# Odd attention: the low keys of each map in a tile of 128 rows, half of them zero

## The chip, the cores and the metric

The kernel runs on one core of a Trainium2 chip. The metric is device time of one execution in microseconds (us). A core has TensorE (PE; its weight loads are shown as PEld), VectorE (DVE), ScalarE (ACT), GpSimd (POOL) and SyncE (SP), which here only issues transfers. Each engine takes its instructions in program order; they wait for each other by semaphores.

## The reference

A float32 model of three layers for 512 tokens of 1024 features. The first layer mixes with two softmax attentions and the second with differential attention (the odd mixer); each is followed by a gated feed-forward network with a convolution. The third has a gated delta rule and a squared-relu network. The change touches the differential attention alone. It has 8 heads; each has two maps of queries and keys of 64 features and one set of values of 128:

```python
l1 = jnp.einsum('bqhd,bkhd->bhqk', q1b, k1).astype(jnp.float32) * scale + alibi
l2 = jnp.einsum('bqhd,bkhd->bhqk', q2b, k2).astype(jnp.float32) * scale + alibi
p = (jax.nn.softmax(jnp.where(mask, l1, NEG_INF), axis=-1)
     - lam * jax.nn.softmax(jnp.where(mask, l2, NEG_INF), axis=-1)).astype(v.dtype)
return jnp.einsum('bhqk,bkhd->bqhd', p, v)
```

The output of each head goes through an RMS norm, and all heads through one projection of 1024 x 1024.

## The kernel before, in words

Every large product works on float32r, a form of float32 that holds fewer bits. An operand is split exactly into a high part (a copy, by ScalarE) and a low part (the difference, by VectorE or at some places GpSimd), and a product is the sum of three: high x high, high x low, low x high (`mm3`, L171 to L175). Weights come by DMA of 512 KB into one of two raw tiles and are split into one of four pairs `whi`, `wlo`.

The stage of the odd attention works head by head. For each head `project` (L921) makes keys and queries of both maps, features on the 128 partitions: map 0 in rows 0 to 63 and map 1 in rows 64 to 127. There are 16 steps of three products (the tile `kq`), and they are not done at once but serve as filling: `fill(n)` puts a few of them between the steps of the head before, whose chain of softmax work they cover.

A score is the sum of the same three parts, but with 64 features two of them fit into one product. For map m the tile `qs[:, m]` holds the queries' high part in m's own 64 rows (`r`) and their low part in the other 64 (`ro`); `ks[:, m]` holds the keys' high part in both halves. One product over all 128 rows (L966, the high product) gives high x high + low x high. The third part, the queries' high part by the keys' low part, is a second product (L967, the low product) that adds into the same bank. Before the change it takes the 64 rows `r` alone, of `qs` and of a tile `kl` in which both maps' low keys lie one above the other; `kl` has two buffers, used by the heads in turn.

`scores(qb)` (L959) does this for one block of 128 queries, for map 0 and then map 1, with 256, 256, 384 and 512 columns of keys for the blocks 0 to 3. Each score then goes through one operation on VectorE (L970: the position's bias and the row's minimum), an exponential on ScalarE (L971), the combination of both maps on VectorE (`combine`, L980 to L983), transposes on TensorE (`turn_P`, L392), a copy on ScalarE, and the product with the values (`pv`, L992). The head's output is normed (GpSimd, L1005 to L1008), scaled (`o`, L1014), transposed (`ot`, L1019) and split in the course of the next head.

The order of all this on TensorE, ScalarE and VectorE is written out by hand (L1040 to L1115, `manual_schedule`). The keys' low parts of the next head are written by `k_lo` (L938), directly after `scores(3)`. In the last head there are no next keys, and products of the output's projection (`o`) serve as filling. GpSimd splits one weight tile a head, copies the keys' high part to the other half (L936) and makes the bias (L953).

Of the kernel before, what the change touches and what calls it, by code (L numbers as in the profile page):

```python
# [19 lines left out]
S = 512  # L20
D = 1024
P = 128
# [15 lines left out]
class Out:  # L38
    """tokens @ W for 1024 output columns, each block's halves in two of the eight banks, chunk by chunk"""
# [25 lines left out]
def parts(hi, lo):  # L65
    """chunk k of a feature-major pair, for the tokens of block t"""
    return lambda k, t: (hi[:, k, t * P:(t + 1) * P], lo[:, k, t * P:(t + 1) * P])


class Kern:  # L70
# [22 lines left out]
    def open_x(self):  # L93
        """the residual stream and the scratch beside it, at the far end of SBUF"""
        self.xp = self.tc.alloc_tile_pool(name="xp", bufs=1, side="right", reuse_waits="tile")
        self.sp = self.xp
        self.x = self.xp.tile([P, NT, D], F32, name="x")
# [18 lines left out]
    def ps(self, tag, name="ps"):  # L116
        """one PSUM bank; each of the four tags rotates over two"""
        return self.psum.tile([P, 512], F32, tag=tag, name=name, bufs=2)
# [8 lines left out]
    def junk(self):  # L127
        """where squares go that only their sums are wanted of"""
        return self.sp.tile([P, D], BF16, tag="junk", name="junk")

    @contextmanager
    def smalls(self, pool):
        """small tiles come from this phase's pool meanwhile"""
        kept, self.small = self.small, pool
        yield pool
        self.small = kept
# [9 lines left out]
    def split(self, hi, lo, src, eng=None):  # L146
        """src = hi + lo exactly; hi and lo are float32r."""
        i = self.nc.scalar.copy(hi, src)
        return i.ins, (eng or self.nc.vector).tensor_tensor(lo, src, hi.bitcast(F32), ALU.subtract).ins
# [14 lines left out]
    def wsteps(self, raw, n=1024, eng=None):  # L164
        """a weight tile's high part, and the step that makes its low part"""
# [11 lines left out]
    def lnexp(self):  # L177
        """from here on the scalar engine's Exp and Ln come from one table set"""
        self.tc.keep_in_program_order(self.nc.scalar.preload_act_table_set("natural_log_exp_and_others"))

    def rstd(self, ss, n, name="rstd"):
        """1 / sqrt(ss / n + eps) for a small tile of sums of squares."""
# [14 lines left out]
    def scale(self, t):  # L197
        """1 / rms of block t of x"""
# [4 lines left out]
    def prenorm(self, i):  # L203
        """rms_norm of x with gain i, into feature-major parts in hT, in steps for block t"""
# [29 lines left out]
    def postnorm_add(self, gain_row):  # L234
        """x[t] += rms_norm(ps) * gain, ps: two banks of 512 columns; in steps for proj_out"""
# [37 lines left out]
    def proj_A(self, ps, w, M, nk, rhs, cols=slice(0, S), woff=0):  # L273
        """ps[:M, cols] = W_tile^T @ rhs; W tile is [P, nk, M], features land on partitions"""
# [8 lines left out]
    def proj_B(self, ps, t, ws, kper, N, lhs, ks=None, nk=KC):  # L283
        """ps[:, :N] = tokens of block t @ W; W tiles are [P, kper, N]"""
# [7 lines left out]
    def proj_out(self, out, finish, nxt=None, tail=4):  # L292
        """tokens @ W for 1024 output columns; the last `tail` chunks go block by block.
        finish: steps that take a block's sums; nxt: what follows, (i, head): the norm before it, and the
        weights (source, columns) and the products of what goes ahead with two blocks. Or a function of t"""
# [90 lines left out]
    def transpose_P(self, PT, Pt, qb, name, copy=None):  # L386
        """PT[:, kb, qb block] = Pt[:, kb block]^T for kb <= qb"""
# [10 lines left out]
    def head_pair(self, pp, score, v, vcol):  # L398
        """softmax(causal(scores)) v of two heads in stages, by query block and head; score(ps, qb, j, n): the products"""
# [31 lines left out]
        def pv():  # L431
            """(P v)^T, one head in each half of the array's columns"""
# [9 lines left out]
    def even_mixer(self, gain_post, nxt):  # L442
        nc, a = self.nc, self.a
        with self.pool("ev_o") as op_:
            # outputs: fox heads as parts, MLA heads for now as they are
# [13 lines left out]
    def _even_attention(self, pp, fox, oT, out):  # L459
# [7 lines left out]
        # running sums of the forget gates: parts, and those of their negatives  # L467
# [5 lines left out]
        # fox values, token-major  # L473
# [11 lines left out]
        # fox heads' parts, two heads at a time: high and low above one another; high parts of the keys twice;  # L485
        # high parts of the queries and low parts of the keys, under them the gates' sums' parts against ones
# [13 lines left out]
        # shared rotary keys and forget gates  # L500
# [72 lines left out]
        # compressed queries and keys, normed token-major, then feature-major  # L573
# [38 lines left out]
        def flat(blocks, late=None):  # L612
            """the blocks' products and sums of squares; what follows apart or, with some that are late, behind six
            products of the next block"""
# [15 lines left out]
        # (the rotations' tables carry the scale)  # L630
# [9 lines left out]
        class Head2:  # L640
            """the queries and keys of two MLA heads"""
# [46 lines left out]
        with self.tc.manual_schedule(engines={E.PE, E.Activation, E.DVE}):  # L688
            # fox heads
# [106 lines left out]
        # MLA heads; a pair's last transposes and its products with the values are in the next one  # L796
# [82 lines left out]
    def _odd_attention(self, pp, ohi, olo, out):  # L879
# [32 lines left out]

        ws, w_lo = {}, [nothing] * 20
# [7 lines left out]
        def project(h):  # L921
            """steps to the parts of both maps' keys and queries: keys' high parts twice, queries' parts one
            above the other"""
            qs = pp.tile([P, 2, S], F32R, tag="qs", name="qs", bufs=2)
            ks = pp.tile([P, 2, S], F32R, tag="ks", name="ks", bufs=2)
            kl = pp.tile([P, S], F32R, tag="kl", name="kl", bufs=2)
            heads[h] = qs, ks, kl
# [10 lines left out]
            def k_lo():  # L938
                for m, (r, ro) in enumerate(rows):
                    nc.vector.tensor_tensor(kl[r], pk[r], ks.bitcast(F32)[r, m, :], ALU.subtract)  # L940
# [8 lines left out]
        def attend(h):  # L949
            """scores (negative) and probabilities, in stages: scores by block, transposes by block, products by block"""  # L950
            qs, ks, kl = heads[h]
# [7 lines left out]
            def scores(qb, between=nothing):  # L959
# [4 lines left out]
                for m in range(2):  # L964
                    ps = self.ps("a", "sc")
                    mm(ps[:, :w], qs[:, m, qb * P:(qb + 1) * P], ks[:, m, :w], start=True, stop=False)  # L966
                    mm(ps[:, :w], qs[rows[m][0], m, qb * P:(qb + 1) * P], kl[rows[m][0], :w], start=False, stop=True)  # L967
# [30 lines left out]
            def norm():  # L998
                # rms_norm of po / den
# [118 lines left out]
    def head_A(self, srcs):  # L1118
        """the first half of the tokens for the first four tiles of features"""
# [12 lines left out]
    def head_B(self, srcs):  # L1132
        """the first two blocks of a token-major product"""
# [6 lines left out]
    def head_block(self, t, ws=None):  # L1140
        """block t of a token-major product, from the head if it is there"""
# [6 lines left out]
    def dn_head(self):  # L1148
        """halves of the gates' tile and of the first keys and queries"""
# [49 lines left out]
    def deltanet(self, nxt):  # L1199
        nc, a = self.nc, self.a  # L1200
        self.spill_x()
        with self.pool("dn_o") as op_:
            # w and the decayed q of each block; then, in their place, the parts of its gated outputs
# [4 lines left out]
            with self.pool("dn") as pp, self.smalls(pp):  # L1208
                hd = [dict(h=h, wq=[w[:, h] for w in wq]) for h in range(8)]
                with self.pool("dn_t") as tp:  # L1210
# [5 lines left out]
                    # v, then u, then the outputs  # L1216
# [24 lines left out]
    def _dn_tail(self, sp, pp, st, hd, new_parts, nw):  # L1241
        """u and w, the scan over the chunks, gates, and the outputs' parts"""
# [7 lines left out]
        # q's scale 1 / sqrt((|q|^2 + eps) dk) goes to the outputs  # L1250
# [13 lines left out]
        # what the scan's waits are filled with, and the number of blocks it needs the parts of  # L1264
# [47 lines left out]
    def _dn_gates(self, tp, pp, st):  # L1312
        """per-token decay and step sizes of all heads, token-major [P, block, head]"""
# [50 lines left out]
        def soft(y, sign, out):  # L1364
            """out = max(sign*y, 0) + ln(1 + exp(-|y|))"""
# [31 lines left out]
        # rows of gc, as exact bfloat16 parts, for broadcasting over partitions  # L1397
# [12 lines left out]
        # and of its exponential  # L1410
# [8 lines left out]
    def _dn_conv(self, st, h, i, c):  # L1419
        """projection and causal convolution of one head's q, k or v, feature-major"""  # L1420
# [16 lines left out]
    def _dn_qk(self, tp, pp, st, d):  # L1437
# [11 lines left out]
        # products of keys with keys and queries, and of queries, within the chunks  # L1449
# [10 lines left out]
        # sums of squares per token lie on the diagonals  # L1460
# [6 lines left out]
        # rho = beta / (|k|^2 + eps), in logarithms  # L1467
# [6 lines left out]
        # decays within the chunks, masked: [key, block, query in its chunk]  # L1474
# [8 lines left out]
        # decayed queries  # L1483
# [23 lines left out]
    def _dn_solve(self, tp, st):  # L1507
        """inverses of the 32-wide unit triangles on the diagonals, one per partition"""
# [14 lines left out]
        # columns of the inverse are independent: two engines take some each  # L1523
# [14 lines left out]
    def _dn_post(self, tp, pp, st, d):  # L1538
        """inverses of the 64-wide triangles from those of their halves, then u and w"""
# [78 lines left out]
    def _dn_z(self, sp, t, ws):  # L1618
        """silu of the gates' projection for four heads of a block"""
# [18 lines left out]
    def _dn_norm(self, sp, st, t, half):  # L1638
        """scales of four heads' outputs in a block: the norm's joined with q's"""
# [13 lines left out]
    def _dn_parts(self, st, t, half, z, r, gp, nw):  # L1653
        """the parts of rms_norm(o) * silu(z) for four heads of a block, feature-major"""
# [39 lines left out]
def build(nc, tc, a):  # L1694
    with ExitStack() as ctx:
# [40 lines left out]
        def final(t, ps):  # L1736
            """out = rms_norm(x + ps), by halves"""
# [19 lines left out]
def pack_A(w, cols):  # L1757
    """[K, N] -> tile [128, K/128 * len(cols)]: W[k*128+p, cols[c]] at [p, k, c]"""
# [5 lines left out]
def pack_B(w, kper):  # L1764
    """[K, N] -> tiles [K/(128 kper), 128, kper*N]"""
# [46 lines left out]
def pack(inp):  # L1812
# [6 lines left out]
    # layer 0  # L1819
# [20 lines left out]
    # layer 1  # L1840
# [6 lines left out]
    # FFN  # L1847
# [6 lines left out]
    # gated deltanet and MLP  # L1854
# [28 lines left out]
```

## Time and profile before

| what | value |
|---|---|
| timed runs | 1982.19 us median of 3 (1981.41 to 1982.5) |
| profiled execution | span 1982.6 us; the record has no time beside the span |
| TensorE busy | 1951.9 us, 98% |
| weight loads busy | 1587.0 us, 80% |
| VectorE, ScalarE, GpSimd busy | 1011.6, 823.1, 253.0 us |
| chain that ended last | 84% TensorE |
| stage of the odd attention | 705.7 to 866.1 us |

The busy time of TensorE counts matmuls whose ends are modelled, and a matmul's end overlaps the start of the next. How long one holds the engine is therefore read from its start to the start of the next. The notation 64*128 64x256 in a row means 64 rows by 128 columns of the array, and a moving operand of 64 x 256.

### The profile page before, as it was taken

To read this page: it belongs to the slowest core of one execution; us is meant where nothing else is said; L and a number is where in the kernel's file an instruction comes from. 1 tells how busy PE (TensorE), PEld (TensorE's weight loads), DVE (VectorE), ACT (ScalarE), POOL (GpSimd) and SP (SyncE) were. 2 spreads that over 40 slices of the span, in tenths; PEclk is the share of its full clock that TensorE was granted. 3 is DMA by queue.
4 is the path that set the end of the run, shared out by engine and by line. 5 is a ranking of instruction groups with operands and counts; after the bars stand their busy time and mean duration, and the time that the engine had idled before them with its cause. 6 is when DMAs were issued, how large, how long until landed. Compare 5 with 4: busy or idle time off the path is not lost.

```text
span 1982.6 us, 25298 instructions
## 1 busy us (share of the span) xinstructions
PE 1951.9 (98%) x9960; PEld 1587.0 (80%) x9960; DVE 1011.6 (51%) x1663; ACT 823.1 (42%) x1411; POOL 253.0 (13%) x336
## 2 busy tenths in 40 slices
PE   8999999999999999999999999999999999999998
PEld 6787688888888777778888888888778888888886
DVE  5666665444323546747444432577764645324423
ACT  4656544333313455645333321476532334313322
POOL 0213210000000233311000000100353310000000
PEclk9999999999999999999999999999999999999999
DMA  5111133322221411123323322323330143322322
GB/s 172 58 65 64 43 108 109 103 97 96 96 96 64 136 54 48 60 75 108 98 97 102 96 96 88 113 98 103 93 96 1 51 141 107 96 96 96 96 96 75
DMA packets 51643, 177.76 MB, mean 90 GB/s; under 512 B 7188, under 2 KB 8084, under 8 KB 51396
## 3 DMA queue, kind: packets, MB, share of 16 engines
q1 hardware_dynamic: 50068, 173.38, 26.7%
q0 software_dynamic: 1456, 2.76, 0.5%
q8 instruction: 79, 1.29, 0.3%
q14 instruction: 40, 0.33, 0.0%
HBM read 170.28 MB, written 5.77 MB: 89 GB/s over the span
## 4 chain that ended last, share of the span: by engine, by line
PE 84%; DVE 4%; ACT 2%; issue 1%; DMA 1%; POOL 0%; POOLq 0%; ACTq 0%; DVEq 0%
PE o L173 9%; PE o L174 9%; PE o L175 9%; PE gate L173 4%; PE val L175 4%; PE val L173 4%; PE gate L175 4%; PE gate L174 4%; PE val L174 4%; PE up L175 3%; PE up L174 3%; PE up L173 3%; PE kq L173 2%; PE dproj L173 2%; PE dproj L175 2%; PE dproj L174 2%
## 5 line engine op out<-in xcount | busy, mean ns | idle before, releaser
L169 DVE TENSOR_TENSOR wlo<-raw,whi 128x1024 fp32r<-128x1024 f32 (+1 forms) x277 | 341.0, 1232 | 553.1 <-ACT whi L168 548.6
L168 ACT CAST whi<-raw 128x1024 fp32r<-128x1024 f32 (+1 forms) x301 | 313.9, 1044 | 620.6 <-PE o L175 283.9
L173 PE MATMUL o<-whi,ahi 128*128 128x512 f32 x352 | 139.4, 396 | 0.0
L174 PE MATMUL o<-wlo,ahi 128*128 128x512 f32 x352 | 139.0, 395 | 0.0
L175 PE MATMUL o<-whi,alo 128*128 128x512 f32 x352 | 139.0, 395 | 0.0
L173 PE MATMUL gate<-hhi,whi 128*128 128x512 f32 x320 | 124.5, 389 | 0.0
L174 PE MATMUL gate<-hlo,whi 128*128 128x512 f32 x320 | 124.5, 389 | 0.0
L175 PE MATMUL val<-hhi,wlo 128*128 128x512 f32 x320 | 124.5, 389 | 0.0
L175 PE MATMUL gate<-hhi,wlo 128*128 128x512 f32 x320 | 124.5, 389 | 0.0
L173 PE MATMUL val<-hhi,whi 128*128 128x512 f32 x320 | 124.5, 389 | 0.0
L174 PE MATMUL val<-hlo,whi 128*128 128x512 f32 x320 | 124.5, 389 | 0.0
L173 PE MATMUL o<-whi,mhi 128*128 128x512 f32 x288 | 113.8, 395 | 0.0
L175 PE MATMUL o<-whi,mlo 128*128 128x512 f32 x288 | 113.6, 395 | 0.0
L174 PE MATMUL o<-wlo,mhi 128*128 128x512 f32 x288 | 113.6, 394 | 0.0
L188 POOL TENSOR_TENSOR po_rr<-po_ru,mhalf 128x1 f32<-128x1 f32 x16 | 8.7, 541 | 763.8 <-DVE po_ru L187 763.8
L175 PE MATMUL up<-hhi,wlo 128*128 128x512 f32 x224 | 87.3, 390 | 0.0
L173 PE MATMUL up<-hhi,whi 128*128 128x512 f32 x224 | 87.2, 389 | 0.0
L174 PE MATMUL up<-hlo,whi 128*128 128x512 f32 x224 | 87.1, 389 | 0.0
L175 PEld LDWEIGHTS o<-whi,alo 128*128 128x128 f32 x352 | 66.0, 187 | 16.2
L173 PEld LDWEIGHTS o<-whi,ahi 128*128 128x128 f32 x352 | 66.0, 187 | 16.0
L174 PEld LDWEIGHTS o<-wlo,ahi 128*128 128x128 f32 x352 | 66.0, 188 | 15.9
L174 PE MATMUL head<-hlo,whi 128*128 128x256 f32 (+1 forms) x256 | 72.3, 284 | 0.0
(413 smaller groups left out, 4423.8 us busy)
## 6 DMA issues: line engine op xcount, KB each, us to landing
raw<-in_ff_wup SPq DMA_DIRECT2D x88, 512.0 KB, 3.5
raw<-in_ff_wdown SPq DMA_DIRECT2D x44, 512.0 KB, 3.5
raw<-in_ml_wup SPq DMA_DIRECT2D x32, 512.0 KB, 3.5
raw<-in_ml_wdown SPq DMA_DIRECT2D x32, 512.0 KB, 3.5
raw<-in_dn_wqkv SPq DMA_DIRECT2D x24, 512.0 KB, 3.6
raw<-in_od_wqk SPq DMA_DIRECT2D x16, 512.0 KB, 3.6
raw<-in_ev_wqk SPq DMA_DIRECT2D x8, 512.0 KB, 3.5
raw<-in_ev_wout SPq DMA_DIRECT2D x8, 512.0 KB, 3.6
```

What stands on the lines that cost most here:

```text
L168: self.nc.scalar.copy(hi[:, :n], raw[:, :n])
L169: return (hi, lo), lambda: (eng or self.nc.vector).tensor_tensor(lo[:, :n], raw[:, :n], hi.bitcast(F32)[:, :n], ALU.subtract)
L173: mm(out, lhs[0], rhs[0], start=start, stop=False)
L174: mm(out, lhs[0], rhs[1], start=False, stop=False)
L175: return mm(out, lhs[1], rhs[0], start=False, stop=stop)
L188: nc.gpsimd.tensor_tensor(r, u, self.mhalf.to_broadcast([P, w]), ALU.pow)
```

## The change

The tile `kl` gets a half for each map and all 128 rows. The rows that a map doesn't use are set to zero once, ahead of the heads, and the low product runs over all 128 rows: the queries' low part meets zeros. There is one `kl` for all heads in place of two buffers. Its size in a partition is the same, 2 x 512 values. (Comments and docstrings were taken out in the same edit. From L913 on, the lines of the changed kernel are numbered 3 higher.)

```diff
         rows = [(slice(64 * m, 64 * m + 64), slice(64 - 64 * m, 128 - 64 * m)) for m in range(2)]
         heads = {}
 
+        kl = pp.tile([P, 2, S], F32R, name="kl")
+        for m, (r, ro) in enumerate(rows):
+            self.tc.keep_in_program_order(nc.vector.memset(kl.bitcast(F32)[ro, m, :], 0.0))
+
...
             ks = pp.tile([P, 2, S], F32R, tag="ks", name="ks", bufs=2)
-            kl = pp.tile([P, S], F32R, tag="kl", name="kl", bufs=2)
-            heads[h] = qs, ks, kl
+            heads[h] = qs, ks
...
             def k_lo():
                 for m, (r, ro) in enumerate(rows):
-                    nc.vector.tensor_tensor(kl[r], pk[r], ks.bitcast(F32)[r, m, :], ALU.subtract)
+                    nc.vector.tensor_tensor(kl[r, m, :], pk[r], ks.bitcast(F32)[r, m, :], ALU.subtract)
...
-            qs, ks, kl = heads[h]
+            qs, ks = heads[h]
...
                     mm(ps[:, :w], qs[:, m, qb * P:(qb + 1) * P], ks[:, m, :w], start=True, stop=False)
-                    mm(ps[:, :w], qs[rows[m][0], m, qb * P:(qb + 1) * P], kl[rows[m][0], :w], start=False, stop=True)
+                    mm(ps[:, :w], qs[:, m, qb * P:(qb + 1) * P], kl[:, m, :w], start=False, stop=True)
```

On TensorE, ScalarE and GpSimd the same instructions stand in the same order. On VectorE two are added. The first place is ahead of the heads, behind the small operations on lambda. Before:

```order
L149 TENSOR_TENSOR hlo<-pn_t,hhi 128x4x128 x4
L895 TENSOR_TENSOR lam<-lam 128x128
L896 TENSOR_REDUCE lam_s<-lam 128x2
L900 SCALAR_TENSOR_TENSOR nlam<-lam_e 128x1
L169 TENSOR_TENSOR wlo<-raw,whi 128x1024 x3
L940 TENSOR_TENSOR kl<-kq,ks 64x512 x2
```

Now:

```order
L149 TENSOR_TENSOR hlo<-pn_t,hhi 128x4x128 x4
L895 TENSOR_TENSOR lam<-lam 128x128
L896 TENSOR_REDUCE lam_s<-lam 128x2
L900 SCALAR_TENSOR_TENSOR nlam<-lam_e 128x1
L915 MEMSET kl 64x512 x2
L169 TENSOR_TENSOR wlo<-raw,whi 128x1024 x3
L943 TENSOR_TENSOR kl<-kq,ks 64x512 x2
```

The memsets stand between the operation on lambda (`nlam`) and three weight splits; the rest is as it was. The second place is on VectorE in the course of head 0, where the keys of head 1 are written, and the numbers behind L and mn are those of buffers. Before:

```order
L970 ISA L_5786,mn_5787<-sc,bias 128x512
L970 ISA mn_5787 128x1
L970 ISA L_5793,mn_5794<-sc,bias 128x512
L970 ISA mn_5794 128x1
L940 TENSOR_TENSOR kl<-kq,ks 64x512 x2
L980 RECIPROCAL ord<-oden 128x2
L982 SCALAR_TENSOR_TENSOR occ<-oden,nlam,ord 128x1
L983 SCALAR_TENSOR_TENSOR L_5786<-L_5793,occ,L_5786 128x512
L945 SCALAR_TENSOR_TENSOR qs<-kq,qs 64x512 x2
```

Now:

```order
L973 ISA L_5787,mn_5788<-sc,bias 128x512
L973 ISA mn_5788 128x1
L973 ISA L_5794,mn_5795<-sc,bias 128x512
L973 ISA mn_5795 128x1
L943 TENSOR_TENSOR kl<-kq,ks 64x512 x2
L983 RECIPROCAL ord<-oden 128x2
L985 SCALAR_TENSOR_TENSOR occ<-oden,nlam,ord 128x1
L986 SCALAR_TENSOR_TENSOR L_5787<-L_5794,occ,L_5787 128x512
L948 SCALAR_TENSOR_TENSOR qs<-kq,qs 64x512 x2
```

Nothing moved here. The two subtractions into `kl` stand behind the reductions of both maps' last scores, now with one buffer for all heads.

## Rows read from the trace of the kernel before

**Rows 1.** The page's first line

```profile
span 1982.6 us, 25298 instructions
```

**Rows 2.** Windows, odd attention: length, PE, PEld, DVE, ACT, POOL busy, clock, DMA share, GB/s

```profile
705.70:866.10 160.40, 160.40 (x761) 119.43 (x760) 106.66 (x275) 96.67 (x267) 52.95 (x63) 1.00 0.19 60
```

**Rows 3.** Timeline of TensorE, head 0 and 1: start, length, engine, line, tiles, rows*columns

```profile
707.95 0.28 PE L966 MATMUL sc<-ks,qs 128*128 128x256 f32 x1
708.15 0.38 PE L967 MATMUL sc<-kl,qs 64*128 64x256 f32 x1
708.47 0.50 PE L173 MATMUL kq<-hhi,whi 128*128 128x512 f32 x1
708.80 0.39 PE L174 MATMUL kq<-hlo,whi 128*128 128x512 f32 x1
709.03 0.40 PE L175 MATMUL kq<-hhi,wlo 128*128 128x512 f32 x1
...
709.96 0.28 PE L966 MATMUL sc<-ks,qs 128*128 128x256 f32 x1
...
711.44 0.39 PE L174 MATMUL kq<-hlo,whi 128*128 128x512 f32 x1
...
739.44 0.49 PE L967 MATMUL sc<-kl,qs 64*128 64x512 f32 x1
...
741.05 0.40 PE L174 MATMUL kq<-hlo,whi 128*128 128x512 f32 x1
```

**Rows 4.** Timeline of TensorE, scores of the attention before, all of 128 rows

```profile
83.51 0.28 PE L568 MATMUL sc<-ks,qs 128*128 128x256 f32 x1
83.63 0.28 PE L569 MATMUL sc<-k,q 128*128 128x256 f32 x1
83.75 0.23 PE L409 MATMUL sc<-maskb,identb 128*128 128x128 bf16 x1
```

**Rows 5.** Timeline of the weight loads around one lone pair

```profile
708.15 0.18 PEld L967 LDWEIGHTS sc<-kl,qs 64*128 64x128 f32 x1 [0.24 <-issue]
...
708.57 0.19 PEld L174 LDWEIGHTS kq<-hlo,whi 128*128 128x128 f32 x1
```

**Rows 6.** Groups on VectorE, a memset: form, count | busy, mean ns | idle before

```profile
L493 DVE MEMSET q<- 32x1024 f32 x2 | 1.8, 912 | 0.5 <-issue 0.5
```

**Rows 7.** Timeline of VectorE ahead of the odd attention's scores

```profile
671.87 2.21 DVE L169 TENSOR_TENSOR wlo<-raw,whi 128x1024 fp32r<-128x1024 f32 x1 [6.09 <-ACT whi L168]
```

**Rows 8.** Timeline of VectorE, head 1

```profile
732.28 0.69 DVE L1014 TENSOR_TENSOR o<-pv,or 128x512 f32<-128x512 f32 x1 [0.56 <-POOL or L1008]
...
733.34 2.71 DVE L983 SCALAR_TENSOR_TENSOR L<-L,occ,L 128x256 f32<-128x256 f32 x1
...
740.82 0.69 DVE L970 CUSTOM_DVE_ANT_0 L<-sc,bias 128x512 f32<-128x512 f32 x1 [0.15 <-PE sc L967]
...
741.43 0.68 DVE L940 TENSOR_TENSOR kl<-kq,ks 64x512 fp32r<-64x512 f32 x1
```

**Rows 9.** Timeline of GpSimd, head 1

```profile
733.38 2.37 POOL L169 TENSOR_TENSOR wlo<-raw,whi 128x1024 fp32r<-128x1024 f32 x1 [1.13 <-ACT whi L168]
```

**Rows 10.** Timeline of TensorE, the output's transposes in head 1

```profile
734.20 0.27 PE L1019 MATMUL ot<-ident,o 128*128 128x128 f32 x1
```

**Rows 11.** Windows, two stretches of the first layer

```profile
216.00:220.00 4.00, 2.17 (x9) 1.51 (x9) 3.61 (x8) 2.19 (x7) 2.15 (x2) 0.87 0.47 152
220.00:224.00 4.00, 4.00 (x20) 3.25 (x19) 1.36 (x7) 1.80 (x6) 0.00 (x0) 0.71 0.03 13
```

**Rows 12.** Timeline of TensorE in the first of them

```profile
218.64 0.54 PE L674 MATMUL sc<-k,q 96*128 96x128 f32 x2 [1.83 <-ACT P L416]
```

**Rows 13.** Timeline of VectorE, last head

```profile
854.92 0.51 DVE L983 SCALAR_TENSOR_TENSOR L<-L,occ,L 128x256 f32<-128x256 f32 x1
855.35 0.54 DVE L970 CUSTOM_DVE_ANT_0 L<-sc,bias 128x384 f32<-128x384 f32 x1
```

**Rows 14.** Timeline of TensorE, transposes of block 1, last head

```profile
857.03 0.27 PE L392 MATMUL ptr<-ident,L 128*128 128x128 f32 x1
```

## The prediction, as put on record before the changed kernel ran

> **What bounds the kernel now.** I looked first at the table of windows over the program's stages, because a change of one stage is worth what that stage's limit allows. In the stretch of the odd attention, 705.7 to 866.1 us, TensorE is busy in all 160.4 us, VectorE in 106.66, ScalarE in 96.67 and GpSimd in 52.95; the granted clock is 1.00 and the DMA engines are at 0.19 [rows 2]. So TensorE's own sequence sets the length, and its waits don't show as idle time. The next view is therefore the timeline of TensorE, read from start to start, since a matmul's length contains a pipelined end that the next one covers.
>
> It shows where the time of a score goes. In the lone pair that begins at 707.95 the high product (L966, 128 rows, 256 columns) starts, the low product (L967, 64 rows) 0.20 later, the next projection step (L173) 0.32 after that, and its follower another 0.33 later: 0.85 from the high product to that follower, where a follower of the ordinary kind comes after 0.23 [rows 3]. Two score products of the same 256 columns that both use 128 rows, in the attention of the layer before, start 0.12 and 0.12 apart, and what follows starts on time [rows 4]. The columns that stream are the same; what differs is the number of rows. So the excess is 0.85 - (0.12 + 0.12 + 0.23) = 0.38 us for one low product: about 0.09 before it, 0.19 behind it and 0.10 behind the next instruction.
>
> The weight loads say the same from another side. The load of the low product at 708.15 comes after 0.24 us in which the loading side waited for nothing the profile names, and starts together with its matmul; the load of L174 at 708.57 already runs while the matmul of L173, started at 708.47, streams [rows 3, 5]. Where the number of rows changes, nothing is loaded ahead.
>
> **The change part by part.** *Low products.* There are 64 of them (8 heads, 4 query blocks, 2 maps), and each switches the array to 64 rows and back. Two in a row, as in all blocks but the first, go from 709.96 to 711.44, 1.48 us, where four full products and a projection step would take 4 x 0.12 + 0.23 = 0.71: 0.77 for two. With 512 columns the part from the first low product (739.44) to the second projection step (741.05) takes 1.61 instead of 4 x 0.23 = 0.92; with the 0.09 ahead of the first one that is 0.78 for two, so the excess does not grow with the columns [rows 3]. The new product streams the same columns through 128 rows, between two others of 128 rows, so all of it should go: 64 x 0.385 = 24.6 us. Bounds: nothing, if the excess hangs on something other than the number of rows, and 64 x 0.39 = 25.0.
>
> A rule of the Trainium skill speaks against this: "TensorE: Matmul & The Clock Gate", Part 3, What overlaps and what doesn't, says that a weight load overlaps with a running matmul only when the two use different row groups. By it the full-row load would be exposed, and the sum would be that of the second rival below; the loads of L174 and of the other full products, which run under matmuls of the same rows, disagree with it [rows 3, 5].
>
> *The two memsets* of the unused halves stand on VectorE behind the small lambda operations, and ahead of a weight split that VectorE waits 6.09 us for, until 671.87 [rows 7]. A memset of 32 x 1024 takes 0.91 us [rows 6]; by free size two of 64 x 512 take about 0.9 together, an estimate that lies wholly within those 6.09 us. Cost 0, bound 0.9 if the cover were gone; the scores begin some 34 us later [rows 2]. The memory that they overwrite was the stage before's, and the operations on the last norm's transposes, ahead of them in VectorE's order, come after that stage's last products.
>
> *One buffer instead of two for the low keys.* The subtraction that writes the next head's keys (L940) must now come after the last low product of this head. On VectorE it stands directly behind the reduction of that very score: reduction at 740.82, subtraction at 741.43 [rows 8]. The reduction needs the product itself, so the added wait has always ended. Queued behind it are the combination of block 3, the split of the queries and then the next head's scores, and they lose nothing. Cost 0; a bound below nothing has no reason, since the instruction's size stays 64 x 512. Memory is the same, 4 KB a partition.
>
> *Loads, DMAs and the other engines.* No transfer and no instruction of ScalarE or GpSimd is added or moved. TensorE asks for each weight tile sooner: the stage shrinks by 15%, and DMA at 0.19 can follow [rows 2].
>
> *What is late next.* VectorE's 106.66 us stand against some 136.8 of the shorter stage, 78%, so no engine becomes the bound by sum; single waits may. The nearest in a middle head is the transposition of the attention's output: TensorE reaches it at 734.20 [rows 10], its operand is ready at 732.28 + 0.69 = 732.97 [rows 8], 1.23 us of slack. Four low products lie ahead of it in the head, so TensorE comes 1.54 sooner. If the operand did not move, 0.31 us would be lost, 2.2 in seven heads; but the chain to it begins behind products that follow two of those four and moves by 0.77 at least. I take 0 and keep 2.2 for the range. In the last head fewer projection steps lie between the scores. There the transposes of block 1 start at 857.03 [rows 14], and VectorE has combined that block at 854.92 + 0.51 = 855.43 and then reduces a score until 855.89, which frees the bank that the last scores need [rows 13]. Six low products ahead bring TensorE 2.3 sooner, to 854.7: between nothing (VectorE moves along) and 2.3 is lost again (nothing of the six kept). VectorE goes from one operation to the next there, so some of it is; I take 1.0, near to the 855.89 - 854.7 = 1.2 if it doesn't move.
>
> Sum: 24.6 - 1.0 = 23.6. The profiled span is 1982.6 [rows 1], with nothing else around it in the record; that is 0.4 above the median 1982.19 of the timed runs. 1982.6 - 23.6 = 1959.0, and by the same 0.4 a median of 1958.6 us.
>
> **Rivals.** *Nothing changes* (1982): the excess belongs to the accumulation pair or to taking the same queries twice, not to the rows. For it: both products of a score read one slice of queries. Against it: the pairs of the other attention accumulate in the same way without it, and the excess falls on the instructions after the low product too, which have nothing to do with the scores [rows 3, 4]. The Trainium skill has this as a rule ("TensorE: Matmul & The Clock Gate", Why this matters for your kernels: a single matmul on 32 rows takes the time of one on 128, and the gain of few rows is concurrency); the trace agrees for the streaming alone, and shows the price of changing the rows beside it. Chance 3%.
>
> *The full-row load is exposed.* Each low product would still be held for its own load, 0.19 us [rows 5]: 64 x 0.19 = 12.2 of the gain go, and 1958.6 + 12.2 = 1970.8. Against it are the full products 0.12 apart, whose loads take longer than that [rows 4, 5]. Chance 4%.
>
> *New waits in every head.* The output's transposes wait 0.31 in seven heads and the last head gives back 2.3: 1958.6 + 2.2 + 1.3 = 1962.1; a stretch of half clock may come with it (next), 1963.8. For it: 1.23 us of slack against 1.54. Against it: the chain moves too. Chance 12%.
>
> *Slower: VectorE is held by GpSimd until the clock falls.* One combination took 2.71 us from 733.34 on, while GpSimd split a weight tile from 733.38 for 2.37 [rows 8, 9]; its neighbours take well under 1. With TensorE sooner, the scaling of the output could fall behind that pass in seven heads, 2.4 us each. After 1.83 us of idle TensorE ahead of 218.64 [rows 12] the granted clock was 0.87 and 0.71 in two stretches of 4 us, which is its lower level, 1.2 GHz, for a part of each: (0.13 + 0.29) x 4 = 1.7 us lost [rows 11]. 7 x (2.4 + 1.7) = 28.7 against 23.6: 1987. It decides from 23.6 / 7 = 3.4 us lost in a head, so only if both come nearly every time. Against it: the scaling stands ahead of the pass, by 1.1 us, and both hang on scores that move together. Chance 2%.
>
> **How the numbers follow.** The forecast as worked out has 79%, and about 1956.5 to 1961 for itself. The range of 8 in 10 takes in the waits and part of the exposed loads: 1956 to 1967. A measurement can tell 0.2% (4 us) from no change. Faster by more than that: 79 + 4 + 12 = 95%; within it 3%; slower 2%.
>
> **What would show it.** In the profile after: low products of 128 rows, 0.12 (256 columns) and 0.23 (512) behind the high ones, the next projection step as soon; the first group of steps, L173, no longer longer than its two siblings after a score; each head about 3.1 us shorter; the stage at 137; VectorE's waits for the low products shorter, and small waits of TensorE only near the end of the last head. It is wrong if steps stay 0.3 apart around full-row low products, or if TensorE is idle for tenths of a microsecond ahead of the transposes in each head.

## The result, and the profile after

| what | before | after |
|---|---|---|
| timed runs, median (lowest to highest, runs) | 1982.35 us (1981.41 to 1983.11, 4) | 1962.38 us (1961.50 to 1963.59, 4) |
| ratio, with its 95% interval | | 0.9899 [0.9885, 0.9913] |
| odd attention, first score to last output transpose | 167.74 us | 147.24 us |
| period of a middle head, first score to first score | 20.57 us | 17.67 to 18.06 us |

The kernel is 20.0 us faster, where 23.6 was forecast (1958.6 us, with 1956 to 1967 as the range). The profiled execution took 1961.64 us, of which its span is 1959.9. This is the page's first line.

```profile
span 1959.9 us, 25300 instructions
```

The next row is the view of windows over the odd attention, from the first score product to the start of the last transpose of an output. The columns are length, then the busy time of TensorE, its weight loads, VectorE, ScalarE and GpSimd, the granted clock, the DMA share and GB/s. First the kernel before, then after:

```profile
705.94:873.68 167.74, 167.53 (x796) 125.04 (x795) 107.36 (x276) 98.40 (x276) 54.75 (x68) 1.00 0.18 57
```

```profile
703.88:851.12 147.24, 145.90 (x796) 122.12 (x795) 107.83 (x276) 94.75 (x276) 54.51 (x68) 1.00 0.21 65
```

The stage is 20.5 us shorter with the same number of matmuls. VectorE still does 107 us of work, now in 147, and TensorE has 1.3 us of idle time that the view shows, where it had 0.2.

What the change aimed at came out as forecast. The timeline of TensorE in head 0 answers to [rows 3] (start, length, engine, line, tiles, rows*columns; the lines are 3 higher):

```profile
721.59 0.28 PE L969 MATMUL sc<-ks,qs 128*128 128x256 f32 x1
721.71 0.28 PE L970 MATMUL sc<-kl,qs 128*128 128x256 f32 x1
...
724.11 0.28 PE L969 MATMUL sc<-ks,qs 128*128 128x256 f32 x1
724.22 0.28 PE L970 MATMUL sc<-kl,qs 128*128 128x256 f32 x1
724.34 0.28 PE L969 MATMUL sc<-ks,qs 128*128 128x256 f32 x1
724.46 0.29 PE L970 MATMUL sc<-kl,qs 128*128 128x256 f32 x1
724.59 0.40 PE L173 MATMUL kq<-hhi,whi 128*128 128x512 f32 x1
724.82 0.40 PE L174 MATMUL kq<-hlo,whi 128*128 128x512 f32 x1
```

From the first high product to the second projection step of such a block it is 0.71 us (724.11 to 724.82) where it was 1.48. The weight loads beside a low product no longer stand still. In [rows 5] the load came after 0.24 us of idle time; now it runs while the high product, started at 719.88, streams:

```profile
719.96 0.19 PEld L970 LDWEIGHTS sc<-kl,qs 128*128 128x128 f32 x1
720.09 0.19 PEld L173 LDWEIGHTS kq<-hhi,whi 128*128 128x128 f32 x1
720.20 0.19 PEld L174 LDWEIGHTS kq<-hlo,whi 128*128 128x128 f32 x1
```

To see where the rest went, every instruction of TensorE in the stage was put beside its counterpart, and the time from its start to the start of the next one compared. The sums of the differences, by kind of step:

| step, by the lines of before | times | sum, us |
|---|---|---|
| high product to low product (L966 to L967) | 64 | -8.27 |
| low product to what follows (L967 to L173, L966, L992) | 64 | -12.30 |
| the one behind (L173 to L174, L992 to L992) | | -4.00 |
| to the last transposes of a head (L992 to L392) | 7 | +0.83 |
| to a score behind transposes (L392 to L966) | 16 | +2.19 |
| last head and small ones | | +1.04 |
| all | | -20.51 |

The first three are 24.57, against 24.6 forecast. The other three are 4.06, against 1.0 forecast. Of them 2.4 lie where one middle head ends and the next begins, at one or two places each, and 1.5 in the last head. The two places in head 1, in the timeline of TensorE after the change:

```profile
735.65 1.54 PE L995 MATMUL pv<-v,PT 128*128 128x128 f32 x12
737.22 0.63 PE L392 MATMUL ptr<-ident,L 128*128 128x128 f32 x4
737.94 0.36 PE L969 MATMUL sc<-ks,qs 128*128 128x256 f32 x1
```

The four transposes of block 3 begin 0.31 after the last value product where they began 0.11 after it, and the next head's first score follows the last of them by 0.36 where it was 0.03. Both hang on VectorE, whose timeline over the same head is this:

```profile
727.14 2.46 DVE L985 SCALAR_TENSOR_TENSOR occ<-oden,nlam,ord 128x1 f32<-128x1 f32 x1
729.63 0.48 DVE L986 SCALAR_TENSOR_TENSOR L<-L,occ,L 128x256 f32<-128x256 f32 x1
...
732.02 0.17 DVE L983 RECIPROCAL ord<-oden 128x2 f32<-128x2 f32 x1 [0.29 <-ACT L L974]
732.23 0.22 DVE L985 SCALAR_TENSOR_TENSOR occ<-oden,nlam,ord 128x1 f32<-128x1 f32 x1
...
735.87 0.17 DVE L983 RECIPROCAL ord<-oden 128x2 f32<-128x2 f32 x1 [0.25 <-ACT L L974]
...
736.32 0.75 DVE L986 SCALAR_TENSOR_TENSOR L<-L,occ,L 128x512 f32<-128x512 f32 x1
737.11 0.69 DVE L948 SCALAR_TENSOR_TENSOR qs<-kq,qs 64x512 fp32r<-64x512 f32 x1
```

An operation on 128x1 values takes 2.46 us at 727.14 and 0.22 at 732.23. Beside the long one GpSimd splits a weight tile:

```profile
727.18 2.40 POOL L169 TENSOR_TENSOR wlo<-raw,whi 128x1024 fp32r<-128x1024 f32 x1 [0.87 <-ACT whi L168]
```

Released at 729.60, VectorE works to 737.80 with only the two gaps in these rows, 0.29 and 0.25 us. The combination of block 3 ends at 737.07 and the transposes start at 737.22; the split of the queries ends at 737.80 and the score starts at 737.94. In the kernel before the same hold is in [rows 8] (733.34, 2.71 us), but there the combination ended 1.20 us ahead of the transposes that need it:

```profile
743.31 0.75 DVE L983 SCALAR_TENSOR_TENSOR L<-L,occ,L 128x512 f32<-128x512 f32 x1
```

```profile
745.26 0.60 PE L392 MATMUL ptr<-ident,L 128*128 128x128 f32 x4
```

From the release to those transposes it was 745.26 - 736.05 = 9.21 us before and is 737.22 - 729.60 = 7.62 now; VectorE's work in between, some 6.9 us, did not shrink with it. Up to the end of that combination VectorE needed 744.06 - 736.05 = 8.01 us before and needs 7.47 now, 0.54 less, because it waits less. TensorE's way is 1.59 shorter, and would be 1.79 shorter without its new wait of 0.20. The slack of 1.20, of which 0.15 is left, covered 1.05 of the difference; the other 0.20 is the wait.

In head 2 the hold itself is new. Before, GpSimd's pass was the one that took longer there (2.67 us from 753.95) and VectorE's combination at 753.90 had its usual 0.48; after the change VectorE is held in each of heads 1 to 5.

### The profile page after: what moved, and what is told of

Read it like the earlier page. It is cut to its first block, busy times and chain, and to the rows that moved or that the text cites. A ratio compares the mean times of both kernels' runs of the same rounds, so it can differ in the third digit from the quotient of the medians.

```text
span 1959.9 us, 25300 instructions
## 1 busy us (share of the span) xinstructions
PE 1929.2 (98%) x9960; PEld 1583.7 (81%) x9960; DVE 1012.9 (52%) x1665; ACT 819.2 (42%) x1411; POOL 253.2 (13%) x336
## 4 chain that ended last, share of the span: by engine, by line
PE 52%; DVE 2%; ACT 1%; issue 1%; DMA 1%; POOL 0%; POOLq 0%; ACTq 0%; DVEq 0%
PE o L173 6%; PE o L175 6%; PE o L174 6%; PE up L173 3%; PE up L174 3%; PE up L175 3%; PE gate L174 2%; PE val L174 2%; PE val L175 2%; PE gate L175 2%; PE gate L173 2%; PE val L173 2%; PE dproj L173 2%; PE dproj L174 2%; PE dproj L175 2%
## 5 line engine op out<-in xcount | busy, mean ns | idle before, releaser
L173 PE MATMUL o<-whi,ahi 128*128 128x512 f32 x352 | 139.4, 396 | 0.0
L174 PE MATMUL o<-wlo,ahi 128*128 128x512 f32 x352 | 139.0, 395 | 0.0
L174 PE MATMUL gate<-hlo,whi 128*128 128x512 f32 x320 | 124.5, 389 | 0.0
L173 PE MATMUL gate<-hhi,whi 128*128 128x512 f32 x320 | 124.5, 389 | 0.0
L173 PE MATMUL val<-hhi,whi 128*128 128x512 f32 x320 | 124.5, 389 | 0.0
L174 PE MATMUL val<-hlo,whi 128*128 128x512 f32 x320 | 124.5, 389 | 0.0
L173 PE MATMUL o<-whi,mhi 128*128 128x512 f32 x288 | 113.8, 395 | 0.0
L174 PE MATMUL o<-wlo,mhi 128*128 128x512 f32 x288 | 113.6, 395 | 0.0
L173 PE MATMUL up<-hhi,whi 128*128 128x512 f32 x224 | 87.2, 389 | 0.0
L174 PE MATMUL up<-hlo,whi 128*128 128x512 f32 x224 | 87.2, 389 | 0.0
L174 PEld LDWEIGHTS o<-wlo,ahi 128*128 128x128 f32 x352 | 66.0, 188 | 16.0
L173 PEld LDWEIGHTS o<-whi,ahi 128*128 128x128 f32 x352 | 66.0, 187 | 15.9
L174 PE MATMUL head<-hlo,whi 128*128 128x256 f32 (+1 forms) x256 | 72.3, 284 | 0.0
```

The costliest lines, as they stand in the source:

```text
L173: mm(out, lhs[0], rhs[0], start=start, stop=False)
L174: mm(out, lhs[0], rhs[1], start=False, stop=False)
```

## The experiments

**Only the rows.** The changed kernel with its memsets and its single `kl`, but with the low product on 64 rows again:

```diff
-                    mm(ps[:, :w], qs[:, m, qb * P:(qb + 1) * P], kl[:, m, :w], start=False, stop=True)
+                    mm(ps[:, :w], qs[rows[m][0], m, qb * P:(qb + 1) * P], kl[rows[m][0], m, :w], start=False, stop=True)
```

> The changed kernel with one thing undone: the low product takes only the 64 rows of its own map again, while the one buffer of low keys, the memsets and all the rest stay. If the gain comes from the number of rows (my theory), the time goes back to that of the kernel before, 1982 us within 2, and the timeline of a lone pair shows steps of 0.21, 0.31 and 0.33 us again. If the tile's new form or the single buffer had a part in the gain or in the loss of the last 4 us, the time lies off 1982 by that part: single buffer and memsets cost 0 by my theory; by the rival that they hold VectorE, 1984 or more.

Measured: 1982.97 us (10 runs) against 1983.65 for before on the same chip (13 runs), ratio 0.9999 [0.9990, 1.0008]. The stage is 167.73 us, every head has the length that it had before, and the steps of TensorE are those of [rows 3]:

```profile
706.55 0.28 PE L969 MATMUL sc<-ks,qs 128*128 128x256 f32 x1
706.75 0.38 PE L970 MATMUL sc<-kl,qs 64*128 64x256 f32 x1
707.07 0.50 PE L173 MATMUL kq<-hhi,whi 128*128 128x512 f32 x1
707.40 0.39 PE L174 MATMUL kq<-hlo,whi 128*128 128x512 f32 x1
```

So the number of rows is the whole cause, and memsets and buffer cost nothing that can be measured.

**The same products, fewer changes of rows.** The kernel before, its low products on 64 rows as they were, but in blocks 1 to 3 in the order high, high, low, low, so that the array changes once a block and not twice:

```diff
+                def products(m, part):
+                    if part == 0:
+                        pss[m] = self.ps("a", "sc")
+                        mm(pss[m][:, :w], qs[:, m, qb * P:(qb + 1) * P], ks[:, m, :w], start=True, stop=False)
+                    else:
+                        mm(pss[m][:, :w], qs[rows[m][0], m, qb * P:(qb + 1) * P], kl[rows[m][0], :w], start=False, stop=True)
+                if qb:
+                    for part in range(2):
+                        for m in range(2):
+                            products(m, part)
```

> The kernel before, with the products of a block in another order: high, high, low, low in blocks 1 to 3 of each head (24 pairs) in place of high, low, high, low; the low products keep their 64 rows. If it is the change between 64 and 128 rows that costs, half of those changes go: 24 x 0.39 = 9.4 us, so about 1973, less some wait because the first map's score is complete later. If the two low products, which lie in different rows of the array, also run at the same time, another 0.12 to 0.23 a pair, 4.2 in all: 1969. If products of 64 rows are slow by themselves, nothing: 1982.

Measured: 1970.14 us, ratio 0.9931 [0.9916, 0.9946]; the stage is 154.59 us, 13.15 shorter. The timeline of TensorE shows more than a saved change:

```profile
735.85 0.71 PE L969 MATMUL sc<-ks,qs 128*128 128x512 f32 x2
736.50 0.49 PE L971 MATMUL sc<-kl,qs 64*128 64x512 f32 x2
736.92 0.50 PE L173 MATMUL kq<-hhi,whi 128*128 128x512 f32 x1
737.26 0.40 PE L174 MATMUL kq<-hlo,whi 128*128 128x512 f32 x1
```

Two low products together take 0.49 us, what one takes in [rows 3], starting within 0.01 of each other, and the next step begins 0.42 after them: in different halves of the rows they run side by side. The Trainium skill says that they can ("TensorE: Matmul & The Clock Gate", Why this matters for your kernels), and the trace agrees. A block of 512 columns takes 1.41 us to the second step, where it took 2.02 before and takes 1.24 after the change (731.52 to 732.76). Two changes of the rows in a block cost 2.02 - 1.24 = 0.78. With one change, and one low product hidden behind the other, it is 1.41 against 1.24 - 0.23 = 1.01: 0.40. The stage's 13.15 stands against 9.4 + 4.2 = 13.6 expected.

Two products at once could pay a price of their own only once, so this run alone does not exclude that a 64-row product is slow by itself. The profile of the kernel before speaks against that, in the third layer, where eight products of 64 rows (of float32, not float32r) follow each other:

```profile
1509.97 1.16 PE L1602 MATMUL ds<-u,ktok 64*128 64x128 f32 x8
```

The second starts 0.21 us after the first, and the other six 0.11 after the one ahead; value products of 128 rows and the same 128 columns start 0.11 apart too. Only the first, behind a product of 128 rows, pays. So the price follows the changes of the row count, and 128 rows without any change still beat two 64-row products at once with one change.

That order with full rows in it, as a control on the order alone (the diff is the one above, with `qs[:, m]` and `kl[:, m]`):

> A control for the order high, high, low, low: the changed kernel with that order in blocks 1 to 3, all products on 128 rows. By the theory of the change of rows there is nothing to gain, and two low products of 128 rows are 0.12 to 0.23 apart, not at once as those of 64 rows were: TensorE's steps as in the changed kernel, stage 147.2 us within 1 (the first map's score is complete a step later, the second's unchanged). If the order itself had helped, the stage is several us shorter.

Measured: 1962.05 us in a single run, with a stage of 146.76, 0.5 below the changed kernel's. In this one profile the order by itself is worth half a microsecond; what the experiment before gained came from the rows.

**GpSimd's splits taken away.** To test whether the hold makes the new waits, the changed kernel with the splits that GpSimd did during the heads put on VectorE, which adds work to the engine that is late:

```diff
-                ws[i], w_lo[i] = self.wsteps(self.wload(a["od_wqk"][i ^ 1]), eng=None if i % 2 else nc.gpsimd)
+                ws[i], w_lo[i] = self.wsteps(self.wload(a["od_wqk"][i ^ 1]), eng=None if i % 2 or i >= 4 else nc.gpsimd)
```

> The changed kernel, with the weight split that GpSimd does in each head (from the tile of head 2 on, 6 of them) done by VectorE at the same place of the written order. My theory of the missing 4 us: GpSimd's pass of 2.4 us holds VectorE between the combination of block 1 and the scores of block 2, and the chain behind it (scores 2, ScalarE's dense row of work, combination of block 3, split of the queries) ends 0.2 us late at the last transposes and 0.33 late at the next head's first score. VectorE's own split takes 1.2 instead, so the chain ends 0.9 sooner and both waits go in six heads: 3 us less, about 1959 where the changed kernel has 1962.4. If VectorE's own load is what makes the chain late, its 1.2 us more a head cost 1 us a head: 1968.

Measured: 1960.45 us (1959.83 to 1961.37), ratio 0.9882 [0.9868, 0.9897]; the stage is 144.45, and middle heads take 17.43 (20.57 less 8 x 0.385 is 17.49, a head without a wait). VectorE's timeline in head 1:

```profile
728.11 0.22 DVE L985 SCALAR_TENSOR_TENSOR occ<-oden,nlam,ord 128x1 f32<-128x1 f32 x1
728.37 0.48 DVE L986 SCALAR_TENSOR_TENSOR L<-L,occ,L 128x256 f32<-128x256 f32 x1
728.77 1.22 DVE L169 TENSOR_TENSOR wlo<-raw,whi 128x1024 fp32r<-128x1024 f32 x1
```

The split costs VectorE 1.22 us and frees it of a hold of some 2.2; the waits between the middle heads are gone, and what is left of the 4.06, about 1.4 us, lies at the start of the last head and in it.

**All splits to GpSimd.** The opposite edit: both weight splits of a head on GpSimd (`eng=None if i % 2 and i < 4 else nc.gpsimd`), which takes 1.22 us of work off VectorE in each head and adds a second pass beside it.

> The changed kernel with twice the suspected cost: from the tile of head 1's second half on, GpSimd also does the weight split that VectorE does in each head, behind the first block's scores (6 or 7 more passes of 2.4 us, VectorE 1.2 a head less). If GpSimd's pass holds VectorE, the new pass delays the combination of block 0 or the scores of block 1, the other one ends later too, and TensorE's waits in a head grow from 0.53 to 1 us or more: 1966 or later, with an operation of VectorE drawn out to over 2 us at a second place of each head. If VectorE's own load were the cause, it has 1.2 less and the waits shrink: 1959.

Measured: 1967.41 us, ratio 0.9917 [0.9901, 0.9934]; the stage is 152.62, 5.4 longer than after the change, and in five heads the last transposes start 1.2 to 1.4 us behind the last value product, where it was 0.11 before and 0.31 after the change. GpSimd and VectorE in head 1:

```profile
727.54 2.43 POOL L169 TENSOR_TENSOR wlo<-raw,whi 128x1024 fp32r<-128x1024 f32 x1 [0.88 <-ACT whi L168]
...
734.69 2.38 POOL L169 TENSOR_TENSOR wlo<-raw,whi 128x1024 fp32r<-128x1024 f32 x1 [0.31 <-POOL ks L939]
737.16 1.50 POOL L956 TENSOR_SCALAR bias<-abase 128x512 f32<-128x512 f32 x1
```

```profile
727.49 0.22 DVE L985 SCALAR_TENSOR_TENSOR occ<-oden,nlam,ord 128x1 f32<-128x1 f32 x1
727.75 2.51 DVE L986 SCALAR_TENSOR_TENSOR L<-L,occ,L 128x256 f32<-128x256 f32 x1
...
734.38 1.39 DVE L943 TENSOR_TENSOR kl<-kq,ks 64x512 fp32r<-64x512 f32 x2
736.01 0.17 DVE L983 RECIPROCAL ord<-oden 128x2 f32<-128x2 f32 x1 [0.24 <-ACT L L974]
736.21 0.88 DVE L985 SCALAR_TENSOR_TENSOR occ<-oden,nlam,ord 128x1 f32<-128x1 f32 x1
737.12 1.19 DVE L986 SCALAR_TENSOR_TENSOR L<-L,occ,L 128x512 f32<-128x512 f32 x1
```

Each pass holds whichever combination meets it, to about the end of the pass (730.26 for 729.97, 737.09 for 737.07), while the subtraction at 734.38, which reads one operand from PSUM, takes its usual 1.39 beside the second pass. More work on VectorE helped and less work hurt, so it is the hold and not the amount of work.

**ScalarE's row.** The rival: block 3's exponentials come late because ScalarE makes a weight tile's high part (1.05 us) ahead of them. That step, `w_hi(2 * h + 5)`, was moved from between `combine(2)` and `scores(3)` to ahead of `scores(2)`:

```diff
                     turn_()
+                    w_hi(2 * h + 5)
                     scores(2)
...
                     combine(2)
-                    w_hi(2 * h + 5)
                     scores(3)
```

> The changed kernel, with ScalarE's cast of the second weight tile of each head (1.05 us) moved from between the scores of block 2 and those of block 3 to ahead of the scores of block 2, where ScalarE is idle for 1.9 us. In the profile ScalarE works from 730.7 to 736.7 us without a pause and the exponential of block 3 starts 0.6 after its operand is there. If the chain through ScalarE's row is what is late, it ends 0.6 sooner and the waits of 0.2 and 0.33 a head go: 3 us less, about 1959. If the hold of VectorE by GpSimd alone sets the end of the chain, nothing changes: 1962.

Measured: 1961.46 us, ratio 0.9889 [0.9873, 0.9906]; the stage is 146.63, 0.6 shorter than after the change where this theory wanted 3. The waits ahead of the transposes are about halved in sum (0.44 us for 0.83), but the score behind them still follows by 0.36 in five heads, since VectorE, released at 729.52, has one gap of 0.30 us until its split of the queries. So ScalarE's order is a small part.

**The last head.** On top of the kernel without GpSimd's splits, one more split of the output's weights on VectorE, and `w_lo[19]` moved behind `scores(3)`:

```diff
                     fill(4)
-                    w_lo[19]()
                     scale_()
...
                     scores(3)
+                    w_lo[19]()
                     fill(2)
```

> The version with the six splits on VectorE, and two more moves for the last head: the split of the projection's second weight tile goes from GpSimd to VectorE too (it held the combination of block 3 in head 6), and the split of the fourth tile, 1.2 us on VectorE, goes from between the scores of block 2 and the scaling of the output to behind the scores of block 3. TensorE waits there now 0.28 at the last head's first score, 0.28 at its block 3 and 0.52 ahead of the transposes of block 2, 1.1 in all. If these come from VectorE's row as in the other heads, about 1.0 goes: the stage 143.5 instead of 144.45 us, some 1959.5. If the chain through ScalarE sets them, the stage stays at 144.4.

Measured: 1961.67 us, ratio 0.9888 [0.9873, 0.9903]; the stage is 143.86, 0.6 shorter and close to what was expected, but that is no gain. TensorE's order came out different in the last head: the stage has 788 matmuls where it had 796, and eight products of the projection run behind the last transposes instead. Up to the projection's last product it is 167.2 us from the first score, where the kernel without GpSimd's splits takes 166.8. The wait at the last head's start is gone, and a product waits for the split that was moved:

```profile
839.40 0.51 PE L174 MATMUL o<-wlo,ohi 128*128 128x512 f32 x1 [1.51 <-DVE wlo L169]
```

In time it can't be told from the kernel without GpSimd's splits, whose median, 1960.45, is the lowest of all. Against the changed kernel that one has 2.8 us in the stage for it; the two ratios' intervals overlap, so by timed runs alone the order of the two is not settled.

## Why the prediction was right or wrong

The time, 1962.38 us, lies inside the range of 1956 to 1967, but above the 1956.5 to 1961 in which the forecast as worked out was to fall.

*The low products* were right, in mechanism and in size: 24.57 us of 24.6 in the steps around them, and nothing is left when the rows are put back. That the full-row loads would be exposed, the second rival, is refuted by the loads that run under the matmul before (719.96 beside 719.88). The rule of the Trainium skill that was weighed against the change ("TensorE: Matmul & The Clock Gate", Part 3, What overlaps and what doesn't) is not borne out for loads into the same rows.

*The memsets and the single buffer* cost nothing, as forecast. The memsets ran at 663.74 for 1.11 us (0.9 was estimated), long ahead of the scores, and VectorE waits 4.96 us behind them:

```profile
663.74 1.11 DVE L915 MEMSET kl<- 64x512 f32 x2
669.82 2.21 DVE L169 TENSOR_TENSOR wlo<-raw,whi 128x1024 fp32r<-128x1024 f32 x1 [4.96 <-ACT whi L168]
```

*What is late next* is the step that failed. The prediction looked at one wait of a middle head, the transposes of the output, and rightly found that their chain moves along: they start at 727.48, and their operand is ready at 726.34 + 0.69 = 727.03.

```profile
726.34 0.69 DVE L1017 TENSOR_TENSOR o<-pv,or 128x512 f32<-128x512 f32 x1 [1.02 <-POOL or L1011]
```

```profile
727.48 0.60 PE L1022 MATMUL ot<-ident,o 128*128 128x128 f32 x4
```

From that one place it took 0 for all middle heads. The place that was missed stood in its own rows: VectorE held by GpSimd for 2.71 us [rows 8, 9]. That hold was read only as a step towards a lower clock, in the slower rival. A hold is no longer than before, and no clock falls in the stage. What shrinks is the time in which VectorE can catch up behind it, by 1.6 us a head, and 1.20 of slack at the transposes of block 3 was all there was. Measured: about 2.4 us in the middle heads, where 0 was taken and 2.2 was the bound, at another place. One of the prediction's own signs of being wrong appeared: in four heads TensorE waits 0.2 us more ahead of the transposes of block 3. Middle heads are 2.5 to 2.9 us shorter instead of 3.1, and the stage up to 866.1, as the prediction counted it, comes to 160.4 - 20.5 = 139.9 instead of 137.

*The last head* gave back 1.5 us where 1.0 was taken, in waits for VectorE: 0.25 and 0.34 at its first two scores, 0.28 at the first score of block 3, and 0.52 at the transposes of block 2.

```profile
834.75 0.50 PE L969 MATMUL sc<-ks,qs 128*128 128x512 f32 x1
...
838.21 0.52 PE L392 MATMUL ptr<-ident,L 128*128 128x128 f32 x3 [0.35 <-DVE L L986]
```

Only the one at block 3 is of the kind that the term was worked out for: that score, right behind the transposes of block 1, waits until VectorE's reduction frees its bank. It has 0.28 where up to 1.2 was reckoned; the others had no term.

Together 23.6 - 20.5 = 3.1 us, most of the 3.8 between forecast and median; the rest is within the scatter of the timed runs. The rival *new waits in every head* had the right time, 1962.1, by luck: it put 2.2 us at the output's transposes, which did not wait, and 2.3 in the last head.

*The profiled execution.* The prediction took the span before, 1982.6, as 0.4 above the median. The records of the later runs give span and time of one execution, 1.7 to 2.1 us apart, so that execution was about 2 us above the median. The forecast did not suffer, since it goes from median to median; the difference of the two spans, 22.7 us, would have been taken for too much (below).

## What to carry to other kernels

Read the price of a small matmul from start to start of its neighbours, with the number of rows beside it: here padding with zeros to 128 rows cost no streaming time and took away the change. When a bottleneck engine gets faster by a known sum, go through every place where it waits for a given engine, and ask at each how long that engine needs since its last forced stop, not only how full it is on average. An operation that takes several times as long as its neighbours in the trace of before (here 2.71 us for 0.48) is a delay that need not shrink with the rest, and a faster engine uses up the slack behind it first.

## What the runs showed of the hardware

Beside a weight split the hold of VectorE by GpSimd is complete, not a slowing: 0.22 us becomes 2.46 for 128 values. It met only operations that take all their operands from SBUF (`occ`, the combinations, and VectorE's own split at 669.82, 2.21 us for 1.22), not those with one operand in PSUM, as at 734.38 above. The Trainium skill has this in "SBUF — State Buffer", Who interferes with whom: a VectorE instruction with two inputs in SBUF contends with a GpSimd instruction that reads SBUF, and the contention is an exclusive lock. The trace agrees for the splits. Beside GpSimd's bias operation it shows a slowing instead: the combination of block 3 at 737.12 takes 1.19 us, where it takes 0.75 at 736.32, and ends 0.35 ahead of the bias operation.

The granted clock does not fall every time. In both profiles TensorE idles for 1.83 us near 218 us; before, 0.87 and 0.71 of the clock were granted behind it [rows 11, 12], after the change all of it, with the same idle time:

```profile
218.35 0.49 PE L674 MATMUL sc<-k,q 96*128 96x128 f32 x2 [1.83 <-ACT P L416]
```

```profile
216.00:220.00 4.00, 2.17 (x13) 1.57 (x12) 3.47 (x9) 2.48 (x8) 1.95 (x1) 1.00 0.43 132
220.00:224.00 4.00, 4.00 (x25) 2.54 (x26) 1.92 (x7) 3.00 (x10) 0.00 (x0) 1.00 0.00 0
1416.00:1420.00 4.00, 1.19 (x6) 0.69 (x5) 3.93 (x9) 0.93 (x2) 3.37 (x9) 0.89 0.44 131
1420.00:1424.00 4.00, 4.00 (x15) 3.35 (x15) 3.90 (x9) 1.23 (x2) 3.37 (x9) 0.68 0.00 0
```

The first score starts 2.1 us sooner in the profile after, most of which that explains (1.7 by the prediction's reckoning), and this has nothing to do with the change (among the runs built on the changed kernel the first score starts anywhere from 703.8 to 706.2): it is the part of 22.7 that the stage's 20.5 doesn't hold. The last two rows show a stretch at the lower level, 1.2 GHz, in the profile after that the one before lacks. VectorE is busy nearly throughout it, and from the stage to the program's end both profiles take 1108.7 to 1108.9 us, so there it cost nothing. Compare stages, not spans, where a few microseconds matter.
